# Hybrid decoder trunk, two layers on one core: four tiles for the samples' queries in place of two, and layer 0's compressed keys transposed later in the program

## The chip, the cores and the metric

The kernel runs as one program on one core of a Trainium2 chip. The metric is device time in microseconds (us), as the median of several executions. Durations and waits come from one profiled execution of the kernel before. Its engines: TensorE (PE, with its weight loads as PEld), VectorE (DVE), ScalarE (ACT), GpSimd (POOL) and SyncE (SP). SP issues the plain DMAs in program order, and a DMA that waits for its buffer holds back those behind it on SP; POOL issues the gathers in the same way.

## The reference, cut to what matters

One inference step through two layers, for one prompt of 512 rows and 8 samples of one row each, d_model 1024. In each layer:

- six modulation vectors per token group, `mod = silu(c) @ ada_w + ada_b` (the conditioning: shift1, scale1, gate1, shift2, scale2, gate2);
- `h = rms(x) * (1 + scale1) + shift1`, one projection `h @ w_in` into the columns of three groups of heads: forgetting attention (6 heads), sparse attention (6 heads, 2 key groups), pooling;
- the mixer, for the prompt over its own rows, for each sample over 2048 cached rows in pages;
- `o @ w_out`, a norm, a gate and the residual; then a squared-ReLU MLP of width 4096 in the same frame.

What the change touches is the samples' part of the mixer:

```python
# forgetting attention: s = q.k * SCALE + (cq - ck), softmax, p @ v over 2048 cached rows and the new one
# sparse attention, compressed branch:
kc, vc = blocks(kc_rows), blocks(vc_rows)      # mean of 64 cached rows each: 32 blocks per sample
s = einsum('btkgd,bnkd->btkgn', q5, kc) * SCALE
p = masked_softmax(s); o = p @ vc; imp = sum over the group's heads of p
idx = top 8 blocks by imp                      # these blocks are then attended to row by row
```

## The kernel before, in words

**Chains.** The program is written by generators that yield a cost after each step. `merge` (L118) keeps a virtual time per chain, the sum of its costs divided by its total (`Chain`, L97; the totals stand in L26), and always takes the next step from the chain furthest behind. A chain that yields `None` is blocked, and enters again at the others' virtual time. This sets the program order. A list scheduler with a modelled timeline then fixes the order on each engine: among what it takes to be ready, the earlier in the program goes first, and the `high_priority` blocks shift that (the conditioning's matmuls by 3000 places, the samples' chains by 300). On the chip each engine runs its list strictly in order. Tiles of one tag share a fixed number of buffers and get them in program order.

**Layer 0's chains that matter here.**
- `gemm_chain` (L826, total 506): 21 column tiles of the input projection, costs 5.3 and 0.45 each. `main` (L1548) then waits for the attention, does the second half of the output projection and the MLP in 8 chunks `c`.
- `fox_prompt` and `nsa_prompt`: the prompt's two attentions, on PE, DVE and ACT in alternation. `wout_first` (L1106) follows with the first half of the output projection.
- `ada0` (L1674, total 35): the conditioning parts 2 to 4, 48 weight loads of 256 KB (`wa`, two buffers, L292), each followed by a few matmuls `pada` (L268) and a cost of 0.25. Two loads share one accumulator in PSUM (L287).
- `cmp0` (L1681, total 70): `pre_cmp(0)` (L635) gathers 64 tiles of cached compressed keys and values (`cr`, POOL, L655), cost 0.2 each, and DVE sums them into two tiles `cg` (L645, L647; one tag, two buffers of 2 KB a partition). At its end it halves the sums, scales them to `kvc` (L666, L668), transposes the keys on PE into the PSUM tile `pkc` (L670, L672) and ACT copies them to `kct`.
- `sample` (total 120): `fox_sample` (L1209) takes 32 pairs of gathered tiles `fk` (POOL and DVE multiply with the query tile `qb`, L1230), four pairs to a sample, then `key_sample` (L1401), then the samples' output projection and MLP (`rows_of`).
- `nsa_sample` (L1320): starts, in the program, once `kct` is written; scores the compressed blocks (`psc`, L1331), ranks them and makes the gather indices `ixs` (`pix`, L1385), which `key_sample`'s gathers need.

**Shared buffers.** PSUM tag `n` is one bank. In layer 0 `ada0`'s `pada`, `pkc`, all of `nsa_sample`'s PSUM tiles, the samples' token-major copies and `wout_first`'s accumulators take it in turn, in program order:

```python
banks = dict(g=2, s=2, o=1, v=1, n=1, x=1)              # L172
acc = ps("pada", tag)                                   # L287, tag "n" from ada0
tag = "o" if l else "n"                                 # L639, in pre_cmp
p = ps("pkc", tag)                                      # L670
```

The SBUF tag `prod` (one buffer, so far 3 KB a partition) serves `lf` in `pre_lf` (L620), `scn` and `rr` in `nsa_sample`, the products in `key_sample` and a row copy in `rows_of`. The query tiles `qb` (L1205, 1.5 KB a partition) have two buffers; `load_q(b + 1)` (L1221) is issued on SP when sample b starts. `take` (L1187) lets the fox gathers run up to five tiles ahead (`RING`) once `kct` stands in the program, and three tiles before that, in layer 0. The gathered tiles `cr`, `fk`, `kt` and `st` share five buffers.

**Joining.** Chunks c = 0 to 3 of layer 0's MLP go without the samples' columns; from c = 4 on the samples are joined (L1576), and these chunks stand in the program behind the samples' own MLP rows. `fill` (L1666) then prepares layer 1: `pre_lf(1)`, `pre_cmp(1)`, where sums trail the gathers by three tiles.

Of the kernel before, what the change touches and what calls it, by code (L numbers as in the profile page):

```python
# [9 lines left out]
F32 = mybir.dt.float32  # L10
# [127 lines left out]
def trunk(ctx: ExitStack, tc: tile.TileContext, x_prompt, x_sample, cache_fox_kv, cache_fox_logf, cache_nsa_kv,  # L138
# [16 lines left out]
    wk = ctx.enter_context(tc.tile_pool(name="wk", bufs=2))  # L155
# [18 lines left out]
    def ps(name, tag="g"):  # L174
        return pp.tile([128, 512], F32, name=name, tag=tag, bufs=banks[tag])

    def acp(out, in_, scale=1.0):
        return S.activation(out, in_, AF.Copy, scale=scale)  # L178

    def ring(name, shape=(128, 1536), dt=F32):  # L180
        return big.tile(list(shape), dt, name=name, tag="ring", bufs=RING)
# [453 lines left out]
    def pre_cmp(l, room=lambda: True):  # L635

        tag = "o" if l else "n"  # L639
        trail = []  # L640

        def add(r, g, x):
            x = x.rearrange("p (r c) -> p r c", r=2)[:, :, 0:256]
            if r == 0:
                V.tensor_copy(ys[g], x)  # L645
            else:
                V.tensor_tensor(ys[g], ys[g], x, op=OP.add)  # L647

        ys = [wk.tile([128, 2, 256], F32, name="cg", bufs=2) for g in range(2)]
        for r in range(32):  # L650
            for g in range(2):
                while not room():
                    yield None
                x = ring("cr", (128, 1024))
                G.indirect_dma_start(out=x, out_offset=None, in_=nsa2,  # L655
                                     in_offset=bass.IndirectOffsetOnAxis(ap=idxc[:, l, g:g + 1], axis=0),
                                     element_offset=r * 1024)
                trail.append((r, g, x))
                if l == 0 or len(trail) > 3:
                    add(*trail.pop(0))  # L660
                yield
        for a in trail:
            add(*a)
        kvc = []
        for g in range(2):
            V.tensor_tensor(ys[g][:, 0], ys[g][:, 0], ys[g][:, 1], op=OP.add)  # L666
            y = wk.tile([128, 256], F32, name="kvc", bufs=2)
            V.tensor_scalar(y, ys[g][:, 0], 1.0 / 64, None, op0=OP.mult)  # L668
            kvc.append(y)
        p = ps("pkc", tag)  # L670
        for g in range(2):
            PE.transpose(p[:, g * 128:(g + 1) * 128], kvc[g][:, 0:128], ident)  # L672
        kct = wk.tile([128, 256], F32, name="kct", bufs=1)
        acp(kct, p[:, 0:256])
        pre[l]["kvc"], pre[l]["kct"] = kvc, kct
# [13 lines left out]
    def layer(l, X, hi, lo, rsw):  # L689
# [510 lines left out]
        qb = {}  # L1200

        def load_q(i):

            if i < 16:
                qb[i] = wk.tile([128, 384], F32, name="qb", bufs=2)  # L1205
                src = qscr[l][i % 8:i % 8 + 1, i // 8 * 384:i // 8 * 384 + 384]
                nc.sync.dma_start(qb[i], src.to_broadcast([128, 384]))

        def fox_sample():  # L1209
# [3 lines left out]
            to_tok([("fq", t) for t in range(3)], ztok[0:8, 0:384], "v")  # L1213
            nc.sync.dma_start(qscr[l][:, 0:384], ztok[0:8, 0:384])
            load_q(0)
            accm, todo = {}, []
            for n in range(32):
                b, j = divmod(n, 4)
                if j == 0:
                    if b < 7:  # L1220
                        load_q(b + 1)  # L1221
                    acc = ps("pvf", "v")
                    if b % 2 == 0:
                        nmS = wk.tile([66, 2, 4], F32, name="nmS", bufs=2)
                        lS = wk.tile([128, 2, 4, 6], F32, name="lS", bufs=2)
# [175 lines left out]
        def key_sample():  # L1401
# [7 lines left out]
            for b in range(8):  # L1409
                v = b % 4  # L1410
                if b == 0:
                    load_q(8)
# [253 lines left out]
        def fill():  # L1666
            while "joined" not in ready:
                yield None
            pre_lf(l + 1)
            yield 0.1  # L1670
            for _ in pre_cmp(l + 1):
                yield 0.3
# [6 lines left out]
            yield from ada(1, range(NB, 6), "n", hold=False)  # L1679

        def cmp0():  # L1681
            for _ in pre_cmp(0):
                yield 0.2

        ch_main = Chain(main(), W_G)
        chains = [ch_main, Chain(fox_prompt(), W_F), Chain(nsa_prompt(), W_N), Chain(pool_chain(), 12),
# [6 lines left out]
        if l == 0:  # L1693
            chains += [Chain(ada0(), W_A0), Chain(cmp0(), W_C0)]
# [17 lines left out]
    ys = ring("ys", (8, 1024))  # L1712
# [41 lines left out]
```

## Time and profile before

| | |
|---|---|
| Median of 3 runs | 1987.18 us (1971.4 to 1987.96) |
| Profiled execution: its time | 1987.2 us |
| Profiled execution: span from first to last instruction | 1985.4 us |
| PE busy in the span | 1823.3 us, 92% |
| Mean granted clock of PE | 0.933 |

A view by windows gives, for each stretch, the busy time of each engine with its number of instructions, the granted clock of PE as a share of 2.4 GHz (0.50 is the lower level, 1.2 GHz), and the busy share and rate of the DMA engines. A timeline row gives start, duration, engine, line, operation, output<-inputs, shapes and count, and in brackets the idle time of the engine ahead of it with what ended that. A view of waits gives who waited for whom: us in total, how often, the longest.

### The profile page before, as it was taken

The numbers are of one execution on the slowest core, as the hardware profiler recorded it, in microseconds if no ns is written. First come the engines' busy times: TensorE is split into PE (matmuls) and PEld (weight loads), VectorE is DVE, ScalarE is ACT, GpSimd is POOL, SyncE is SP. The second block draws the span as 40 slices with busy tenths as digits, with TensorE's granted clock in tenths as the row PEclk, the third lists the DMA queues.
The fourth block names the chain that finished last, engine by engine and source line by source line (L and its number), as shares of the span: only waits on it lengthen the run. The fifth ranks groups of instructions, "written<-read, shape, count | busy, mean of one in ns | idle before, by whom it ended". The sixth has DMA issues, their size and how long they took to land. (4 is left out here: it accounts for less than half of the span.)

```text
span 1985.4 us, 37190 instructions
## 1 busy us (share of the span) xinstructions
PE 1823.3 (92%) x13848; PEld 1434.9 (72%) x13848; DVE 1303.3 (66%) x3175; ACT 851.7 (43%) x1994; POOL 660.1 (33%) x542
## 2 busy tenths in 40 slices
PE   6999879897989899999998999979987999999998
PEld 3887745454648787679996787855665888878997
DVE  3678877666677684347667468896658778634555
ACT  3344535452334342233336344546655443423445
POOL 0535444224225550034340146355433655100000
PEclk9999957787989999999999999979998999999999
DMA  8979776457667667899996465545534776684332
GB/s 295 326 260 302 249 244 216 154 191 238 210 229 213 196 184 236 297 314 344 311 319 187 147 216 175 167 146 177 176 101 163 219 203 185 211 293 132 91 91 71
DMA packets 316024, 420.98 MB, mean 212 GB/s; under 512 B 28441, under 2 KB 233979, under 8 KB 315700
## 3 DMA queue, kind: packets, MB, share of 16 engines
q1 hardware_dynamic: 272324, 233.24, 38.0%
q0 software_dynamic: 43520, 185.36, 27.1%
q8 instruction: 110, 1.80, 0.4%
q14 instruction: 70, 0.57, 0.1%
HBM read 397.26 MB, written 21.44 MB: 211 GB/s over the span
## 5 line engine op out<-in xcount | busy, mean ns | idle before, releaser
L336 PE MATMUL pg<-ah,wh 128*128 128x262 f32 (+4 forms) x1792 | 542.9, 304 | 19.1 <-ACT wz L178 4.1
L336 PE MATMUL pg<-al,wh 128*128 128x262 f32 (+4 forms) x1792 | 536.9, 301 | 4.6 <-DVE al L526 2.9
L336 PE MATMUL pg<-ah,wl 128*128 128x260 f32 (+4 forms) x1792 | 535.1, 299 | 5.6 <-DVE wl L245 5.6
L178 ACT ACTIVATE wh<-wr 128x512 fp32r<-128x512 f32 x372 | 233.2, 629 | 437.1 <-PE pg L336 395.7
L336 PE MATMUL pg<-a,wh 128*128 128x262 f32 (+3 forms) x1664 | 379.1, 316 | 7.6 <-DVE a L1603 4.1
L336 PEld LDWEIGHTS pg<-ah,wh 128*128 128x128 f32 x1792 | 343.6, 192 | 49.8 <-issue 19.7
L336 PEld LDWEIGHTS pg<-al,wh 128*128 128x128 f32 x1792 | 343.0, 192 | 27.0 <-issue 9.5
L336 PEld LDWEIGHTS pg<-ah,wl 128*128 128x128 f32 x1792 | 344.2, 192 | 24.8 <-issue 9.9
L245 DVE TENSOR_TENSOR wl<-wr,wh 128x512 fp32r<-128x512 f32 x368 | 270.6, 737 | 110.0 <-ACT wh L178 107.7
L336 PEld LDWEIGHTS pg<-a,wh 128*128 128x128 f32 x1664 | 276.8, 191 | 40.8 <-issue 9.1
L336 PE MATMUL pg<-a,wl 128*128 128x258 f32 (+3 forms) x832 | 258.8, 312 | 0.9 <-DVE wl L245 0.9
L1230 POOL TENSOR_TENSOR fk<-fk,qb 128x768 f32<-128x768 f32 x96 | 182.9, 1909 | 229.6 <-DMA fk<-in_cache_fox_kv_dram,idxf 157.9
L655 POOL DMA_INDIRECT cr<-in_cache_nsa_kv_dram,idxc x128 | 130.1, 1017 | 308.4 <-PE prw L268 133.1
L485 POOL DMA_INDIRECT fk<-in_cache_fox_kv_dram,idxf x128 | 129.7, 1013 | 270.3 <-PE pvf L1238 97.9
L336 PEld LDWEIGHTS pg<-a,wl 128*128 128x128 f32 x832 | 158.5, 191 | 10.3 <-issue 2.5
L1615 DVE TENSOR_TENSOR F<-F,pg 128x258 f32<-128x258 f32 (+3 forms) x188 | 88.2, 473 | 116.6 <-PE pg L336 112.4
L1231 DVE TENSOR_REDUCE S<-fk 128x12 f32<-128x768 f32 x128 | 120.6, 943 | 24.9 <-POOL fk L1230 24.6
L485 POOL DMA_INDIRECT st<-in_cache_nsa_kv_dram,ixs x96 | 102.7, 1070 | 77.4 <-PE pvs L1444 45.3
L1597 ACT ACTIVATE rl<-rl,wb 128x256 f32<-128x256 f32 (+2 forms) x128 | 64.5, 506 | 134.5 <-DVE rl L1596 132.2
L268 PE MATMUL pada<-wa,cT 128*32 128x256 f32 x640 | 98.5, 426 | 21.2 <-DMA wa<-in_w_ada_dram 20.3
L178 ACT ACTIVATE P<-P,st 128x128 f32<-128x128 f32 (+3 forms) x144 | 78.3, 558 | 48.3 <-DVE st L889 23.7
L1652 POOL TENSOR_TENSOR xt<-xt,yt 128x512 f32<-128x512 f32 x2 | 2.5, 1270 | 281.2 <-DVE xt L1654 279.9
(438 smaller groups left out, 2851.9 us busy)
## 6 DMA issues: line engine op xcount, KB each, us to landing
wr<-in_w_ff_dram SPq DMA_DIRECT2D x256, 256.0 KB
wa<-in_w_ada_dram SPq DMA_DIRECT2D x160, 256.0 KB
wrow<-in_w_ff_dram SPq DMA_DIRECT2D x64, 512.0 KB
wr<-in_w_in_dram SPq DMA_DIRECT2D x80, 256.0 KB
out_dram<-kt SPq DMA_DIRECT2D x16, 512.0 KB
wrow<-in_w_out_dram SPq DMA_DIRECT2D x16, 512.0 KB
kt<-in_cache_nsa_win_dram SPq DMA_DIRECT2D x16, 448.0 KB
qb<-qscr SPq DMA_DIRECT2D x32, 192.0 KB
```

The lines of the kernel that those rows point to most:

```text
L178: return S.activation(out, in_, AF.Copy, scale=scale)
L245: V.tensor_tensor(lo, raw, hi.bitcast(F32), op=OP.subtract)
L268: PE.matmul(acc[c * 32:(c + 1) * 32, 0:256], rows[:, k, :], raw[:, (c % 2) * 256:(c % 2 + 1) * 256], start=first, stop=last)
L336: PE.matmul(acc[:, 0:b - a], wt, x(k)[:, a:b], start=n == 0, stop=n == 3 * nk - 1)
L485: G.indirect_dma_start(out=out, out_offset=None, in_=view, in_offset=bass.IndirectOffsetOnAxis(ap=idx, axis=0))
L655: G.indirect_dma_start(out=x, out_offset=None, in_=nsa2, in_offset=bass.IndirectOffsetOnAxis(ap=idxc[:, l, g:g + 1], axis=0), element_offs ...
L1230: (G if i == 0 or l else V).tensor_tensor(kk, kk, qb[b][:, None, :].to_broadcast([128, 2, 384]), op=OP.mult)
L1231: V.tensor_reduce(S4[:, 2 * i:2 * i + 2], kk.rearrange("p r (h d) -> p r h d", d=64), axis=AX, op=OP.add)
L1597: S.activation(r[:, a:e], r[:, a:e], AF.Relu, bias=st["wb"])
L1615: V.tensor_tensor(F[:, m, a:b], F[:, m, a:b], p[:, 0:b - a], op=OP.add)
L1652: G.tensor_tensor(xt[:, b, h], xt[:, b, h], t, op=OP.add)
```

## The change

The two tiles `cg` become the halves of one tile in the tag `prod`, whose buffer grows from 3 KB to 4 KB a partition. The query tiles get four buffers. `pre_cmp` yields once more, with a cost of 10, between the last sum and the halving; in layer 0 that cost counts (10/70 of virtual time), in layer 1 `fill` replaces it with its own 0.3.

```diff
-        ys = [wk.tile([128, 2, 256], F32, name="cg", bufs=2) for g in range(2)]
+        ys = wk.tile([128, 2, 2, 256], F32, name="cg", tag="prod", bufs=1)
+        ys = [ys[:, g] for g in range(2)]
         for r in range(32):
...
         for a in trail:
             add(*a)
+        yield 10
         kvc = []
         for g in range(2):
             V.tensor_tensor(ys[g][:, 0], ys[g][:, 0], ys[g][:, 1], op=OP.add)
...
-                qb[i] = wk.tile([128, 384], F32, name="qb", bufs=2)
+                qb[i] = wk.tile([128, 384], F32, name="qb", bufs=4)
...
         def cmp0():
-            for _ in pre_cmp(0):
-                yield 0.2
+            for c in pre_cmp(0):
+                yield c or 0.2
```

## Rows read from the trace of the kernel before

**Rows 1.** The page: busy time of PE, and the granted clock of PE in 40 slices of the span, in tenths.
```profile
PE 1823.3 (92%) x13848; PEld 1434.9 (72%) x13848; DVE 1303.3 (66%) x3175; ACT 851.7 (43%) x1994; POOL 660.1 (33%) x542
...
PEclk9999957787989999999999999979998999999999
```
**Rows 2.** Windows over four stretches of layer 0: length, then busy time and count of PE, PEld, DVE, ACT, POOL, then granted clock, DMA share and GB/s.
```profile
75.00:195.00 120.00, 119.95 (x943) 99.44 (x944) 95.97 (x257) 54.07 (x130) 50.31 (x44) 1.00 0.88 297
195.00:246.00 51.00, 45.62 (x372) 38.26 (x370) 40.91 (x107) 24.59 (x57) 24.06 (x20) 1.00 0.80 263
246.00:338.50 92.50, 74.40 (x395) 43.95 (x395) 70.87 (x191) 42.79 (x109) 40.63 (x37) 0.63 0.66 218
338.50:478.50 140.00, 121.61 (x771) 67.12 (x771) 86.48 (x229) 60.83 (x169) 46.12 (x36) 0.74 0.57 196
```
**Rows 3.** The same stretches for the instructions on the tile `pada` alone: busy time and count of PE, PEld, DVE, ACT, then clock, DMA share and GB/s of the whole core.
```profile
75.00:195.00 120.00, 11.29 (x80) 2.62 (x80) 4.13 (x10) 0.39 (x1) 1.00 0.88 297
195.00:246.00 51.00, 0.00 (x0) 0.00 (x0) 0.00 (x0) 0.00 (x0) 1.00 0.80 263
246.00:338.50 92.50, 0.00 (x0) 0.00 (x0) 0.00 (x0) 0.00 (x0) 0.63 0.66 218
338.50:478.50 140.00, 19.15 (x120) 4.08 (x120) 5.36 (x13) 0.77 (x2) 0.74 0.57 196
```
**Rows 4.** Timeline of PE, 335 to 348 us: the users of PSUM tag `n` in their order.
```profile
336.19 0.33 PE L672 MATMUL pkc<-cst,kvc 128*128 128x128 f32 x1
338.67 0.47 PE L672 MATMUL pkc<-cst,kvc 128*128 128x128 f32 x1 [2.15 <-DVE kvc L668]
...
341.07 0.84 PE L1126 MATMUL ptt<-cst,zs 128*8 128x128 f32 x3
...
344.49 1.11 PE L1331 MATMUL psc<-kct,qc 128*64 128x256 f32 x2
...
347.37 1.08 PE L268 MATMUL pada<-wa,cT 128*32 128x256 f32 x8
```
**Rows 5.** The matmuls of the conditioning that read `wa`, 0 to 195 us: count, minimum, median and longest in ns, first and last start in us.
```profile
L268 PE MATMUL pada<-wa,cT x104: 379/403/632, 51.0 to 191.5; 128*32 128x256 f32 x104
```
**Rows 6.** Timeline of DVE, 336 to 339 us: the end of the sums and what is made of them.
```profile
336.70 0.69 DVE L647 TENSOR_TENSOR cg<-cg,cr 128x512 f32<-128x512 f32 x1 [1.16 <-DMA cr<-in_cache_nsa_kv_dram,idxc]
...
338.33 0.28 DVE L668 TENSOR_SCALAR kvc<-cg 128x256 f32<-128x256 f32 x1
```
**Rows 7.** Waits of PE, 338.7 to 478.5 us: us in total, times, longest.
```profile
PE pada L268 <- DMA wa<-in_w_ada_dram: 10.0, 4, 4.9
PE psS L874 <- ACT P L888: 2.5, 3, 2.1
```
**Rows 8.** Timeline of PE: two of these waits.
```profile
395.79 0.63 PE L268 MATMUL pada<-wa,cT 128*32 128x256 f32 x4 [2.99 <-DMA wa<-in_w_ada_dram]
...
438.69 0.62 PE L268 MATMUL pada<-wa,cT 128*32 128x256 f32 x4 [1.81 <-DMA wa<-in_w_ada_dram]
```
**Rows 9.** Windows over three stretches at the lower clock: length, busy time and count of PE, PEld, DVE, ACT, POOL, then clock, DMA share, GB/s.
```profile
338.30:358.80 20.50, 19.82 (x76) 9.45 (x76) 11.94 (x34) 7.90 (x26) 6.51 (x5) 0.50 0.61 220
...
396.40:406.60 10.20, 10.20 (x56) 6.28 (x55) 2.57 (x10) 4.03 (x9) 2.87 (x3) 0.50 0.43 140
...
440.70:447.50 6.80, 6.80 (x41) 3.61 (x40) 3.61 (x8) 1.17 (x4) 0.45 (x1) 0.50 0.18 66
```
**Rows 10.** Waits of SP over the whole span for a buffer of `qb` (L1207): us in total, times, longest.
```profile
SPq L1207 <- DVE fk L1230: 66.5, 7, 47.5
...
SPq L1207 <- POOL fk L1230: 56.9, 5, 43.6
...
SPq L1207 <- DVE prod L1430: 18.0, 8, 3.2
```
**Rows 11.** Timeline of SP: the last load of `wa` ahead of the pause, the load of `qb` behind SP's longest wait for its buffer, and the next loads of `wa`.
```profile
192.95 1.53 SPq L293 DMA_DIRECT2D wa<-in_w_ada_dram  x1
...
342.44 0.36 SPq L1207 DMA_DIRECT2D qb<-qscr  x1
...
348.48 10.41 SPq L293 DMA_DIRECT2D wa<-in_w_ada_dram  x4
```
**Rows 12.** The fox multiplies of layer 0 on POOL, one to a pair, up to 340 us and from 340 to 600 us: count, ns, first and last start.
```profile
L1230 POOL TENSOR_TENSOR fk<-fk,qb x12: 1812/1824/2344, 109.1 to 328.7; 128x768 f32<-128x768 f32 x12
...
L1230 POOL TENSOR_TENSOR fk<-fk,qb x20: 1804/1818/2373, 343.4 to 573.6; 128x768 f32<-128x768 f32 x20
```
**Rows 13.** The indices for the samples' chosen blocks: made, and first used by a gather.
```profile
L485 POOL DMA_INDIRECT kt<-in_cache_nsa_kv_dram,ixs x16: 942/950/1427, 587.9 to 719.5; - x16
L1390 DVE TENSOR_SCALAR ixs<-pix,cst x1: 274/274/274, 416.5 to 416.5; 128x64 int32<-128x64 f32 x1
```
**Rows 14.** Layer 1's preparation: first sums of `cg`, the last reader of `lf`, and the first use of the transposed keys (last start of the row).
```profile
L645 DVE COPY cg<-cr x2: 419/420/421, 872.6 to 875.3; 128x512 f32<-128x512 f32 x2
...
L628 DVE TENSOR_TENSOR tt<-bi,lf x2: 202/206/209, 74.0 to 905.6; 128x48 f32<-128x48 f32 x2
...
L1331 PE MATMUL psc<-kct,qc x4: 379/530/686, 344.5 to 1238.8; 128*64 128x256 f32 x4
```
**Rows 15.** Where the samples' columns are put into the MLP's input (first of the two starts is layer 0), and the first evacuation with the samples joined.
```profile
L611 DVE TENSOR_TENSOR al<-catp,ah x2: 219/222/225, 800.2 to 1737.8; 128x64 fp32r<-128x64 f32 x2
...
L1599 ACT ACTIVATE rl<-pg x16: 155/158/160, 852.3 to 1041.1; 128x8 f32<-128x8 f32 x16
```

## The prediction

> **What bounds the kernel now.** I read the page first: PE is busy for 92% of the span, and its clock is full except in two places, of which layer 0's, around 250 to 480 us, is the larger [rows 1]. So time is won only where PE idles or runs at the lower clock. The windows show where: until 195 us PE is busy without a break at clock 1.00; from 246 to 338.5 us it idles for 92.5 - 74.4 = 18.1 us and has a mean clock of 0.63, from 338.5 to 478.5 us for 18.4 us at 0.74 [rows 2]. The reader is to see next what is missing there. The conditioning's matmuls on `pada`, which need nothing but their weights, run 20 loads in 75 to 195 us, none at all from 195 to 338.5 us, and 30 loads in the 140 us after that (4 matmuls a load) [rows 3]. The timeline says why: `pkc`, then the samples' query copy `ptt`, then `psc`, then `pada` again at 347.37 us, all on the one bank `n` and in program order [rows 4]. In the program `pkc` stands behind 64 gathers of 0.2 at a total of 70, at virtual time 0.183; `ada0` has then issued 0.183 x 35 / 0.25 = 25.6 loads, and the trace has 104 / 4 = 26 before the pause [rows 5]. On the chip the gathers end only at 336.7 us [rows 6]. So a transposition that nobody needs yet holds the bank for which PE's best filler waits, for 150 us.
>
> **The change part by part.** The profiled execution took 1987.2 us (span 1985.4 and 1.8 around it), the median is 1987.18, so sums stand against 1987.2 directly.
>
> *The later step.* A cost of 10 puts halving, scaling, transposition and all behind it at virtual time 0.183 + 10/70 = 0.326. `ada0` is then at 0.326 x 35 / 0.25 = 45.6 loads: 20 of its remaining 22 move ahead of `pkc`. What moves itself is small: four DVE instructions, two transposes, one ACT copy, and `nsa_sample` with its two stores on SP; no gather moves, since the cost comes after the last sum.
> 1. PE stands at `pkc` for 2.15 us because it reached it before the sums were done [rows 4, 6]. Later in the program it is taken when ready: -2.2 (ends: 0 and -2.2).
> 2. Twenty loads leave 338.5 to 478.5 us, where one costs 19.15 / 30 = 0.64 us: -12.8 (the two at 347.37 us took 1.08 us together, which would make 10.8). Ahead, at the pace of 75 to 195 us (one in 6 us, 11.29 / 20 = 0.56 us each), some 8 run in 195 to 246 us, where PE idles for 5.4 us, and 12 in 246 to 338.5 us, where it idles for 18.1 us. I charge 3 of the first 4.8 us and 2 of the other 6.5: +5.0 (ends: 0, all in gaps; +11.3, none).
> 3. With the burst gone its waits for weights go. Of the 10.0 us of such waits in the later stretch [rows 7], those at 395.8 and 438.7 us, 2.99 and 1.81 us, are `ada0`'s own [rows 8]: -4.8 (ends: 0, if they come back earlier; -10.0, if all four go).
> 4. Clock. Right behind these three waits of PE the lower level stands for 20.5, 10.2 and 6.8 us, in which PE is busy for 36.8 us [rows 9]; at 2.4 GHz that is 18.4 us less at most. Other waits, such as 2.5 us on `P`, remain there [rows 7], so I take half, 9.2. In 246 to 338.5 us the filler may lift the clock toward 0.74: 74.4 x (1 - 0.63 / 0.74) = 11 at most, of which I take 2. The later stretch loses filler and may fall toward 0.63: (121.6 - 12.8) x (0.74 / 0.63 - 1) = 19 at most, of which I take 3. Together -8 (ends: -29 and +19).
>
> The Trainium skill, "TensorE: Matmul & The Clock Gate", in Part 1 on the clock gate, says that the throttled state is the default and that activity releases it. The trace agrees: 1.00 in the stretch without gaps, 0.63 in the one with most. By that rule alone the clock term is a transfer of filler from one stretch to the other and its sum would be near 0, so 1974 in place of 1966.
>
> *Four query tiles.* With two, `load_q(b + 1)` waits on SP for the multiplies of sample b - 1: 141 us in all, the longest 47.5 us [rows 10]. That one stands from 295 to 342 us, with the next `wa` loads behind it [rows 11]. In the kernel before nobody misses them, because `pada` waits for bank `n` anyway: 0 by itself. In the changed kernel they are wanted just then, and two buffers would starve term 2 of some 8 loads (47 / 6). With four, a tile's last reader lies three samples back, so the wait is gone. Number and size of the loads stay the same.
>
> The Trainium skill, "DMA: Bandwidth & Descriptors", under "Issuing engines are not separate DMA queues", says that transfers issued by SP and by GpSimd share the same DMA engines and interleave. That speaks against the change: 12 loads of 256 KB are 3.1 MB more beside the gathers between 246 and 338.5 us, 14 us at the 218 GB/s measured there, while the DMA engines are 0.66 busy [rows 2]. By that rule the last sum comes some us later, which after the move holds up nothing on PE.
>
> *Three tiles ahead for longer.* `take` now runs three tiles ahead, not five, for (0.326 - 0.183) x 120 / 1.32 = 13 more pairs of `fox_sample`. Before 330 us, with three and with `cmp0`'s gathers between, a pair took (328.7 - 109.1) / 11 = 20.0 us; after 343 us, with five and alone, 230.2 / 19 = 12.1 us [rows 12]. No row separates the two causes: the ends are 0 and 13 x 7.9 = 103 us on the samples' chain. I expect near the lower end, since the five physical buffers stay and only the gathers' place in the program moves: +2 on PE.
>
> *The index chain.* `pix` now stands behind `wout_first`'s accumulators on bank `n` (its first step is at virtual time 0.389, `pix` at about 0.43). The indices are made at 416.5 us and first used at 587.9 us: 171 us of cover [rows 13]. `wout_first`'s work comes after 478.5 us and may push them past 540 us: 0, with some 40 us left.
>
> *The shared buffer.* In layer 1 the first sums, at 872.6 us, must now wait for the last reader of `lf` at 905.6 us, so the gathers stop after five: up to 33 us on them. The transposed keys made from them are first used at 1238.8 us [rows 14]: 0. In layer 0 the same order costs at most a few us at 60 us, before the pause: 0.
>
> Sum: -2.2 - 12.8 + 5.0 - 4.8 - 8 + 2 = -20.8, and 1987.2 - 20.8 = 1966.4. What is late next is the prompt's attention itself, through `P` and `psT`.
>
> **The rivals.**
> *A. The attention's own chain is the limit.* DVE and ACT alternate with PE in these stretches (DVE 0.77 and 0.62 busy [rows 2]). If PE's relief only widens its gaps, terms 2 to 4 come to 0 and 1985 remains. For it: PE waits on `P` in both. Against: PE is busy for 87% of the later stretch.
> *B. The samples come late (the slower side).* The samples' columns are ready at 800.2 us, and the first joined evacuation is at 852.3 us [rows 15]: 52 us of cover, 32 once the main path is 20 us earlier. Each us per pair on 13 pairs takes 13 us of it. Up to 2.5 us more a pair (14.6) nothing happens; at 4 (16.1) the gain is eaten; at 5.5 (17.6) the end is 20 us later than before, 2007. For it: 20.0 us in the stretch with three tiles. Against: half of the gathers on POOL there were `cmp0`'s.
> *C. The clock goes the other way.* By the rule on activity above, the later stretch, stripped of filler, falls to 0.63, and the earlier one gains nothing. From rows: -20.8 + 8 + 19 = +6, 1993. Against: two of the three stretches at the lower level begin where PE waited for weights of the filler itself.
> *D. It doesn't do what it says:* another user of bank `n` holds `pada` in place of `pkc`. Then terms 2 and 3 go, 1985 as in A; counted with it.
>
> **How the numbers follow.** Chances: forecast 0.53, A with D 0.27, B 0.12, C 0.08. The forecast's own range is 1945 to 1980, from halving and doubling its terms. What a measurement can tell from no change is about 1%, 20 us: below 1967.3 or above 2007.1. Of the forecast four fifths lie below: 0.42 faster. B lies above, beside the tails of A and C and an order of the whole program that the scheduler draws anew: 0.16 slower. The rest, 0.42, is within 1%. For the range, the good ends of all terms give -2.2 - 12.8 - 10 - 29 = -54, or 1933, which I don't expect together; I stop at 1939. Above it must hold A and C and reach into B: 2004.
>
> **What would show it.** Right: `pada` runs all through 195 to 338.5 us, and at most a few of `ada0`'s loads are left after `pkc`; no PE wait at `pkc`; the clock in 246 to 338.5 us is above 0.63; SP's waits for `qb` shrink to a few us; the output projection's first matmul (now 478.5 us) starts some 20 us earlier, and the first joined evacuation too. Wrong: `pada` still pauses (D); it doesn't, and 478.5 us stands all the same (A); the projection is early but the joined evacuation is not (B); the clock after 338.5 us is below 0.7 (C). What would refute the whole: a gain or loss that arises after 600 us, in stages that the change doesn't touch.

## The result: 1.2% slower, and the profile after

| | before | after |
|---|---|---|
| Median | 1987.57 us (4 runs, 1971.4 to 1997.07) | 2010.72 us (4 runs, 2005.39 to 2021.33) |
| Ratio, 95% interval | 1 | 1.0123 [1.0075, 1.0172] |
| Profiled execution, span | 1985.4 us | 2009.1 us |
| Mean granted clock | 0.933 | 0.926 |

The loss to the lower clock, span x (1 - mean clock), is 133 us before and 149 us after; what is left of the span is 1852 and 1860 us. This loss counts PE's idle time at the lower level too. Lines behind L665 lie two higher than before.

The page after, to [rows 1]: as many PE instructions; slices 6 to 12 (layer 0) are better, 16 and 18 (the join, as is seen below), 26 and 28 to 30 (layer 1) and the last worse.
```profile
PE 1841.2 (92%) x13848; PEld 1440.9 (72%) x13848; DVE 1291.6 (64%) x3175; ACT 856.3 (43%) x1994; POOL 666.4 (33%) x542
...
PEclk9999968899999996989999999877888999999998
```
Windows of layer 0 after, to [rows 2]:
```profile
195.00:246.00 51.00, 48.32 (x397) 39.30 (x395) 41.44 (x112) 24.47 (x59) 23.94 (x21) 1.00 0.91 306
246.00:338.50 92.50, 73.89 (x420) 41.25 (x421) 68.72 (x192) 41.75 (x108) 39.29 (x36) 0.70 0.74 249
338.50:478.50 140.00, 133.96 (x887) 84.42 (x886) 95.85 (x242) 76.11 (x195) 45.28 (x36) 0.92 0.59 198
```
The same for `pada` alone, to [rows 3]: 24 + 56 matmuls are 20 loads in what was the pause, and 19 are left in the last stretch.
```profile
195.00:246.00 51.00, 4.34 (x24) 1.08 (x24) 1.24 (x3) 0.00 (x0) 1.00 0.91 306
246.00:338.50 92.50, 10.63 (x56) 2.09 (x56) 2.48 (x6) 0.37 (x1) 0.70 0.74 249
338.50:478.50 140.00, 9.37 (x76) 2.34 (x76) 3.31 (x8) 0.38 (x1) 0.92 0.59 198
```
Timeline of PE after, to [rows 4]: `pkc` is taken without a wait, and the output projection's first matmul stands at 392.88 us, where it was 478.5.
```profile
344.17 0.69 PE L674 MATMUL pkc<-cst,kvc 128*128 128x128 f32 x2
...
349.89 0.42 PE L268 MATMUL pada<-wa,cT 128*32 128x256 f32 x4 [0.52 <-DVE scn L1336]
...
392.88 0.50 PE L336 MATMUL pg<-ah,wh 128*128 128x512 f32 x1
```
So the first part of the mechanism came, and larger than predicted: a lead of 85.6 us. From here on a tile is marked by the moment when ScalarE splits its weights for PE. The lead is 58 us at the MLP's first tile (544.1 to 486.0 us) and 81 us at the last tile of the first product in the MLP's chunk 3 (792.0 to 710.7 us). At the join, right behind that chunk, most of it is lost. First windows of before, then of after, around it:
```profile
700.00:750.00 50.00, 48.18 (x427) 43.28 (x425) 42.61 (x90) 20.62 (x46) 21.63 (x18) 1.00 0.68 193
750.00:800.00 50.00, 49.22 (x394) 38.02 (x395) 22.03 (x60) 13.97 (x33) 0.00 (x0) 1.00 0.71 229
800.00:850.00 50.00, 49.19 (x398) 33.03 (x397) 15.41 (x37) 10.99 (x22) 0.00 (x0) 1.00 0.90 304
850.00:900.00 50.00, 50.00 (x424) 40.41 (x423) 26.68 (x69) 19.87 (x44) 21.46 (x22) 1.00 0.95 321
```
```profile
700.00:750.00 50.00, 48.12 (x404) 42.58 (x404) 40.47 (x86) 20.02 (x47) 29.68 (x26) 1.00 0.68 201
750.00:800.00 50.00, 27.64 (x283) 16.47 (x281) 18.42 (x58) 3.19 (x12) 7.85 (x7) 0.69 0.67 228
800.00:850.00 50.00, 49.65 (x455) 35.69 (x451) 14.70 (x41) 17.44 (x41) 0.00 (x0) 1.00 0.95 332
850.00:900.00 50.00, 41.39 (x310) 31.63 (x306) 21.95 (x58) 7.68 (x15) 21.64 (x23) 0.86 0.78 269
```
After, PE idles 22.4 of the 50 us from 750 us on, at clock 0.69: the MLP has run up to the samples and has nothing to put between. Its last matmul ahead of the join starts at 752.00 us, the next, now with the samples, at 799.39. PE's timeline after shows what runs between, in brackets the idle time and what ended it: the samples' softmax and single loads of the conditioning.
```profile
763.58 0.42 PE L1142 MATMUL pmx<-cst,mx 128*66 128x128 f32 x1 [8.36 <-DVE mx L1137]
...
779.14 1.07 PE L268 MATMUL pada<-wa,cT 128*32 128x256 f32 x4 [3.19 <-DMA wa<-in_w_ada_dram]
...
794.62 0.64 PE L268 MATMUL pada<-wa,cT 128*32 128x256 f32 x2 [4.11 <-DMA wa<-in_w_ada_dram]
...
799.39 0.39 PE L336 MATMUL pg<-ah,wh 128*128 128x260 f32 x1
```
The samples' columns after, to [rows 15]: at 792.0 us, only 8 us sooner than before, and the first joined evacuation 15 us behind them, where it was 52.
```profile
L611 DVE TENSOR_TENSOR al<-catp,ah x2: 224/226/227, 792.0 to 1749.8; 128x64 fp32r<-128x64 f32 x2
...
L1601 ACT ACTIVATE rl<-pg x32: 154/156/158, 807.0 to 1964.1; 128x8 f32<-128x8 f32 x32
```
At layer 0's last tile 18.9 us of the lead are left (1058.95 to 1040.06). In layer 1 they turn into 21.0 us behind at the last tile of the output projection (1486.5 to 1507.5), and the end is 23.7 us late. Windows over layer 1's attention for the tile `pg` alone (input and output projection); the clock is that of the whole core. Before, then after:
```profile
1280.00:1340.00 60.00, 19.74 (x125) 16.87 (x124) 3.14 (x12) 0.32 (x2) 0.79 0.50 158
1340.00:1400.00 60.00, 6.55 (x21) 3.71 (x19) 0.00 (x0) 1.15 (x2) 0.96 0.55 188
1400.00:1460.00 60.00, 18.64 (x72) 12.97 (x72) 0.00 (x0) 2.94 (x5) 1.00 0.33 112
```
```profile
1280.00:1340.00 60.00, 12.26 (x57) 10.49 (x58) 1.60 (x6) 0.15 (x1) 0.67 0.44 141
1340.00:1400.00 60.00, 4.29 (x14) 2.45 (x13) 0.00 (x0) 0.58 (x1) 0.82 0.44 149
1400.00:1460.00 60.00, 13.68 (x53) 9.23 (x51) 0.00 (x0) 2.30 (x4) 0.81 0.29 97
```
Fewer projection matmuls stand beside the attention (124 in place of 218 over the three), and the clock is 0.67 to 0.82 in place of 0.79 to 1.00. A part of this is a shift: the input projection's last weights are split 20 us earlier than before (1299.6 to 1279.6 us), but the attention beside it came later. A matmul that stands in each of its score tiles shows this, before and after, in the first and last start:
```profile
L878 PE MATMUL psS<-cmb,identb x72: 216/229/289, 1159.8 to 1454.5; 128*128 128x128 bf16 x72
```
```profile
L880 PE MATMUL psS<-cmb,identb x72: 219/230/314, 1165.5 to 1474.1; 128*128 128x128 bf16 x72
```
So in layer 1 the lead is one of the projection and not of the attention, which ends 19.6 us later. Of the change only the query tiles are in use here: between 1100 and 1500 us SP waits 42.5 us for one on POOL's multiplies, before 55.6 us. The late step and the tile of the sums are done at 1044 us.

### The profile page after: what moved, and what is told of

Its sections match the earlier page's. It is cut to its first block, busy times and chain, and to the rows that moved or that the text cites. A ratio compares the mean times of both kernels' runs of the same rounds, so it can differ in the third digit from the quotient of the medians.

```text
span 2009.1 us, 37187 instructions
## 1 busy us (share of the span) xinstructions
PE 1841.2 (92%) x13848; PEld 1440.9 (72%) x13848; DVE 1291.6 (64%) x3175; ACT 856.3 (43%) x1994; POOL 666.4 (33%) x542
## 4 chain that ended last, share of the span: by engine, by line
PE 41%; DMA 7%; DVE 6%; issue 3%; POOL 3%; ACT 1%; SPq 0%; DVEq 0%; POOLq 0%; ACTq 0%
PE pg L336 28%; DMA fk<-in_cache_fox_kv_dram,idxf 2%; PE pada L268 2%; DMA wrow<-in_w_ff_dram 2%; PE prw L268 2%; PE ot L908 2%; DMA wa<-in_w_ada_dram 1%; POOL fk L1232 1%; PE psT L901 1%; PE psS L877 1%; DVE S L1233 1%; DVE wl L245 1%; DMA st<-in_cache_nsa_kv_dram,ixs 1%; PE psS L876 1%; PE pvf L1240 1%
## 5 line engine op out<-in xcount | busy, mean ns | idle before, releaser
L336 PE MATMUL pg<-ah,wl 128*128 128x262 f32 (+4 forms) x1792 | 535.0, 299 | 3.2 <-DVE wl L245 3.1
L245 DVE TENSOR_TENSOR wl<-wr,wh 128x512 fp32r<-128x512 f32 x368 | 275.4, 749 | 104.1 <-ACT wh L178 101.9
L1232 POOL TENSOR_TENSOR fk<-fk,qb 128x768 f32<-128x768 f32 x96 | 187.2, 1954 | 269.1 <-DMA fk<-in_cache_fox_kv_dram,idxf 197.8
L1617 DVE TENSOR_TENSOR F<-F,pg 128x262 f32<-128x262 f32 (+3 forms) x188 | 88.1, 473 | 82.7 <-PE pg L336 79.0
L908 PE MATMUL ot<-PT,wz 128*64 128x128 f32 x720 | 98.5, 322 | 2.4 <-ACT PT L178 2.3
```

What stands on the lines that cost most here:

```text
L245: V.tensor_tensor(lo, raw, hi.bitcast(F32), op=OP.subtract)
L336: PE.matmul(acc[:, 0:b - a], wt, x(k)[:, a:b], start=n == 0, stop=n == 3 * nk - 1)
L908: PE.matmul(ot[e * 64:(e + 1) * 64, i * 128:(i + 1) * 128], vs[e](j), PTs[e][:, j * 128:(j + 1) * 128], start=first and j == 0, stop=last ...
L1232: (G if i == 0 or l else V).tensor_tensor(kk, kk, qb[b][:, None, :].to_broadcast([128, 2, 384]), op=OP.mult)
L1617: V.tensor_tensor(F[:, m, a:b], F[:, m, a:b], p[:, 0:b - a], op=OP.add)
```

## The experiments

Theories: **M**, the mechanism just read (late step gives a lead, the join takes it, missing filler in layer 1); **Q**, the buffers cost the time; **S**, every edit makes the list scheduler draw another order, and what that order happens to do in the later stages outweighs the edit. The expectations are in us, with the kernel before at 1987. Runs 1 to 4, 5 to 8, 9 to 12, 13 to 16 and 17 to 18 are groups. In the first and the fourth every kernel, the one before too, took some 3% longer than in the others, so ratios are against the kernel before of the same group. "Loss" is the change of the lower clock's loss in us against it, "rest" that of the remaining span, both means.

| | ratio [95%] | loss | rest |
|---|---|---|---|
| 1 late step alone | 1.0012 [0.9977, 1.0047] | -2 | +5 |
| 2 both buffers alone | 1.0080 [1.0034, 1.0126] | +19 | -6 |
| 3 pause in layer 0 only | 1.0076 [1.0032, 1.0120] | +12 | 0 |
| 4 samples at 100 | 1.0049 [1.0008, 1.0090] | +15 | -4 |
| 6 the whole change | 1.0123 [1.0020, 1.0227] | +14 | +12 |
| 7 shared buffer alone | 1.0176 [1.0097, 1.0254] | +26 | +6 |
| 8 change, join at 7th block | 0.9965 [0.9924, 1.0005] | -6 | -1 |
| 9 shared buffer, `lf` apart | 1.0144 [1.0068, 1.0220] | +21 | +7 |
| 10 null: 505 for 506 | 1.0041 [0.9999, 1.0084] | +16 | -8 |
| 11 null: 121 for 120 | 0.9971 [0.9926, 1.0016] | +6 | -11 |
| 12 late step, join, 90 for 60 | 1.0022 [0.9990, 1.0054] | +2 | +5 |
| 13 shared buffer, first null | 1.0185 [1.0112, 1.0258] | +44 | 0 |
| 14 shared buffer, second null | 0.9975 [0.9931, 1.0019] | -1 | -2 |
| 15 change, first null | 1.0035 [0.9992, 1.0077] | +3 | +4 |
| 16 change, join, tag x | 0.9941 [0.9899, 0.9984] | -19 | +10 |
| 17 as 16 without the change | 1.0109 [1.0068, 1.0151] | +14 | +5 |
| 18 as 16, first null | 0.9995 [0.9951, 1.0039] | -10 | +6 |

**1. The late step alone** (kernel before, with)
```diff
+        yield 10
...
-            for _ in pre_cmp(0):
-                yield 0.2
+            for c in pre_cmp(0):
+                yield c or 0.2
```


> Only the late step: the pause of cost 10 ahead of the transposes in layer 0, two query tiles and two sum tiles as before. Theory M (the late transposes free the PSUM bank, the main path gets 60 to 90 us ahead, loses most of it where the samples join at c=4, and the early-spent products are missing beside layer 1's attention): 2000 to 2015 us, the output projection of layer 0 about 80 us earlier as in the changed kernel, PE idle in 750 to 800 us. Rival Q (four query tiles and the shared sum tile cost the time, in layer 1): 1955 to 1970 us. Rival S (each change of the order redraws the schedule, where it lands is no property of the edit): anywhere in 1970 to 2010 us.


The ratio is 1.0012, neither M's nor Q's. The lead is there (second half of the output projection's weights split at 447.9 us, 447.1 in run 3), with two query tiles; PE is busy for only 121.7 of the 150 us from 750 us on. So the lead is the step's, four tiles aren't needed for it, and in this order nothing of it is left at the end.

**2. The buffers alone**
```diff
-        ys = [wk.tile([128, 2, 256], F32, name="cg", bufs=2) for g in range(2)]
+        ys = wk.tile([128, 2, 2, 256], F32, name="cg", tag="prod", bufs=1)
...
-                qb[i] = wk.tile([128, 384], F32, name="qb", bufs=2)
+                qb[i] = wk.tile([128, 384], F32, name="qb", bufs=4)
```


> Only the four query tiles and the two sums in one tile of the shared buffer; the transposes where they were. M: 1980 to 1995 us, the conditioning pauses in 195 to 338 us as before and the output projection of layer 0 starts near 513 us. Q: 2005 to 2015 us, the loss arising in layer 1. S: 1970 to 2010 us with layer 0's markers as before.


The ratio is 1.0080, without a lead (the same marker stands at 510.6 us), and all of it is loss to the lower clock. That speaks for Q at this point; S allows it too.

**3. The pause in layer 0 alone** (changed kernel, with `if l == 0:` ahead of `yield 10`)


> The changed kernel with the pause of cost 10 in layer 0 alone; in layer 1 the compressed keys are made without it. M: layer 0 as in the changed kernel to within 5 us at every marker, layer 1's attention late again, 2000 to 2015 us. Q: the same, 2005 to 2015 us. S: layer 0 the same, but layer 1 differs by more than 10 us in either direction.


The ratio is 1.0076, within all theories. VectorE, ScalarE and GpSimd have the same instructions in the same order as in the changed kernel, so this is a repetition of it and tests nothing; against run 2 of the same group (1.0080) the late step again makes no difference.

**4. The samples' weight** (changed kernel, `W_S` 120 to 100)


> The changed kernel with the samples' chain given a weight of 100 in place of 120, so that its steps stand earlier in the program. M: the samples' columns of layer 0 (L613 to L616, ready at 792 us in the changed kernel) come before 770 us, PE is busy for more than 40 of the 50 us in 750 to 800 us (27.6 in the changed kernel), total 1985 to 2000 us. Q: no help in layer 1, 2005 to 2015 us. S: 1970 to 2010 us, not tied to the busy time in 750 to 800 us.


The ratio is 1.0049. The expectation has the sign wrong: a smaller total makes the chain's virtual time run faster, so its steps came later (samples' columns at 850.2 us, 823.3 in run 3). 27 us later and not slower: the samples' lateness at the join alone doesn't set the total.

**5, 6. The kernels before and after, once more**


> The kernel before, unchanged, for a profile on the chip of these runs. If the chip alone moved the first four (all 2050 to 2062 us with the kernel before at 2051), its markers lie as in the first profile, stretched by some 3%, with layer 0's output projection again some 60 us later than in the runs that have the late step, and the whole loss to the half clock near 160 us.

> The changed kernel on this chip. If the parts add (late step 1.0012, buffers 1.008 of the kernel before): ratio 1.005 to 1.013. Span less the loss to the half clock within 8 us of that of the kernel before, the loss 12 to 20 us larger, as the buffers alone showed. S (no property of the edit): a ratio anywhere in 0.99 to 1.015.


The kernel before took 1975.6 us in the one execution of run 5: the 3% were the group's, not the kernel's. The change is at 1.0123 again, with a loss 14 us larger, as expected, and a rest 12 us larger, where at most 8 was expected.

**7. The shared buffer alone** (kernel before, the first two lines of run 2's diff)


> Only the two sums in one tile of the shared buffer, two query tiles, no late step. If the shared buffer is what costs in the buffers' part (1.008): ratio 1.005 to 1.011, a mean granted clock below 0.917. If the four query tiles are it: ratio 0.997 to 1.003, clock 0.919 to 0.923.


The ratio is 1.0176, above both expectations and, within the intervals, at least as much as the whole change. **9.** takes `lf` out of the shared buffer:
```diff
-        lf = wk.tile([128, 8, 16, 6], F32, name="lf", tag="prod", bufs=1)
+        lf = wk.tile([128, 8, 16, 6], F32, name="lf", bufs=1)
```


> The sums in the shared buffer, but the gathered forget logs lf in a buffer of their own, so that layer 1's first sums need not wait for lf's last reader; otherwise as the run with the shared buffer alone (1.0176). If that wait is what costs: ratio 0.995 to 1.005, layer 1's sums begin near 872 us again. If the shared buffer costs elsewhere: 1.01 to 1.02. S (each new order lands somewhere): 0.995 to 1.02, with layer 1's sums early and no tie to the time.


Layer 1's first sums, in run 7 and then in run 9:
```profile
L645 DVE COPY cg<-cr x2: 419/419/419, 891.4 to 891.7; 128x512 f32<-128x512 f32 x2
```
```profile
L645 DVE COPY cg<-cr x2: 421/421/421, 857.3 to 857.6; 128x512 f32<-128x512 f32 x2
```
They come 34 us earlier, and the ratio is still 1.0144: the wait for `lf`, the one that the prediction names for this buffer, isn't needed for the loss.

**10, 11. Null changes** (`W_G` 506 to 505; `W_S` 120 to 121)


> A null change of the kernel before: the input projection's total cost 505 in place of 506 (0.2%), which gives each engine another order and nothing else. S: a ratio that differs from 1 by more than its interval, up to 1.015 above or below. M and Q, in which named resources cost the time: 0.997 to 1.003.

> A second null change of the kernel before: the samples' total cost 121 in place of 120 (0.8%). S: a ratio that differs from 1 by more than its interval, up to 1.015 either way, and not that of the first null. M and Q: 0.997 to 1.003.


The ratios are 1.0041 and 0.9971, neither apart from 1 by more than its interval, which S had expected; 1.0041 lies outside what M and Q allow, though its interval reaches into that. Yet both move loss and rest against each other, by +16 and -8, +6 and -11 us.

**13, 14. The shared buffer under the two nulls**


> The shared buffer alone (1.0176) with the first null change (input projection 505 in place of 506). If the shared buffer costs by itself, whatever the order: 1.012 to 1.022. S (the loss belongs to one drawn order): 0.995 to 1.012.

> The shared buffer alone with the second null change (samples 121 in place of 120). Shared buffer by itself: 1.012 to 1.022. S: 0.995 to 1.012, and another ratio than with the first null.


The ratios are 1.0185 and 0.9975. The buffers are the same, costs changed by 0.2% and 0.8%, and 2.1% lie between, with intervals far apart: sharing the buffer is not enough to cost anything, the order that comes with it decides (S). That sharing makes poor orders more likely (runs 7, 9 and 13 against 14) isn't excluded, and the four query tiles were never run alone. **15.** does it to the whole change:


> The whole change (1.0123) with the first null change (505 in place of 506). M, in which the stop at the join and the early-spent products cost the time: 1.008 to 1.017, with PE again idle for more than 15 of the 50 us at 750 to 800 us. S: 0.995 to 1.008.


The ratio is 1.0035, within S's range and not M's, but its interval overlaps that of run 3 (1.0032 to 1.0120), which has the order of the change; so this run leans to S and doesn't show it. The stop at the join is there still (PE busy for 128.9 of the 150 us from 750 us on), though not in the 50 us named.

**8. The join later** (changed kernel; the samples' rows of the MLP compute a third quarter by themselves)
```diff
-SQ = 2, 2
+SQ = 3, 2
```


> The changed kernel with layer 0's samples joined at the seventh and eighth column block in place of the fifth and later (a size: 3 and 2 rows of the schedule in place of 2 and 2), so that the main path meets the samples' chain later; it computes the samples' feed-forward for more blocks by themselves. M: PE no longer stops in 750 to 800 us (over 45 of the 50 us busy), the lead of layer 0's main path is kept to its end, total ratio 0.985 to 1.003. S: 0.995 to 1.015 and no relation to the stop.


The ratio is 0.9965. From 750 us PE no longer stops, and layer 1's first weights are split at 1001.5 us (1053.0 in run 6, 1060.2 in run 5, the kernel before); but there the conditioning isn't ready. First a window, then PE's wait for its loads between 1000 and 1200 us:
```profile
750.00:800.00 50.00, 49.35 (x480) 41.83 (x478) 29.56 (x76) 18.43 (x42) 4.62 (x4) 1.00 0.70 232
```
```profile
PE pada L268 <- DMA wa<-in_w_ada_dram: 18.9, 8, 6.0
```
**12.** tries to bring that forward by its total, on the late step alone (`SQ = 3, 2`, `W_A1` 60 to 90):


> A version: the late step alone (two query tiles, two sum tiles, ratio 1.0012), layer 0's samples joined at the seventh block (ratio 0.9965 with the whole change), and the total of layer 1's conditioning at 90 in place of 60, so that it stands earlier, since in the run with the later join PE waited for its weights at 1112 to 1150 us at half clock (47.8 us). M: 0.975 to 0.99, no stretch at half clock over 20 us in 1050 to 1200 us. S: 0.985 to 1.01.


The ratio is 1.0022, a miss: PE is at half clock for 44.4 us from 1133.6 us on. Behind its first 16 loads, done by 549 us, layer 1's conditioning went on no earlier than in run 8 (777.0 us; 770.7). **16.** takes away what holds it, the users of PSUM tag `s` that stand ahead of it in the program:
```diff
-            tag = "s" if "ff" in ready and feed["w"] % 2 else "x"
+            tag = "s" if l and "ff" in ready and feed["w"] % 2 else "x"
```


> A version: the whole change with the join at the seventh block (0.9965), and the samples' softmax steps of layer 0 on PSUM tag x alone in place of x and s in turn, so that layer 1's conditioning, on tag s, need not wait in program order for the end of the samples' keys (its first product came at 770 us, just as these end). M: the first product of layer 1's conditioning between 530 and 600 us, no half clock of 20 us and more in 1050 to 1200 us, ratio 0.975 to 0.99. S: 0.99 to 1.015.


Windows on `pada`, in run 8 and then in run 16:
```profile
525.00:750.00 225.00, 0.00 (x0) 0.00 (x0) 0.00 (x0) 0.00 (x0) 0.98 0.65 191
750.00:850.00 100.00, 7.78 (x72) 2.29 (x72) 0.00 (x0) 0.39 (x1) 1.00 0.79 266
850.00:1200.00 350.00, 41.67 (x248) 9.35 (x248) 0.00 (x0) 1.55 (x4) 0.90 0.86 293
```
```profile
525.00:750.00 225.00, 33.97 (x232) 7.85 (x232) 0.00 (x0) 1.54 (x4) 0.96 0.72 220
750.00:850.00 100.00, 15.93 (x104) 3.65 (x104) 0.00 (x0) 0.77 (x2) 0.95 0.64 201
850.00:1200.00 350.00, 0.00 (x0) 0.00 (x0) 0.00 (x0) 0.00 (x0) 0.98 0.83 275
```
It is done 300 us earlier, and no stretch at half clock beyond 10.2 us is left from 1050 to 1200 us. The ratio is 0.9941, its interval just below 1, and short of the 0.975 to 0.99 expected. **17, 18.** the same without the change, and under the first null:


> The version of the run before (0.9941) without the change: the join at the seventh block and the samples' softmax steps of layer 0 on tag x, on the kernel before (two query tiles, two sum tiles, no late step). If the late step's lead of 80 us is worth something once the join no longer eats it: 0.998 to 1.008 here, above 0.9941. If the lead is worth nothing: 0.988 to 0.997.

> The version (0.9941) with the first null change (505 in place of 506). If its gain comes from the two edits: 0.988 to 0.998. S, in which it is one more drawn order: 0.998 to 1.012.


Without the change the ratio is 1.0109, above even the 0.998 to 1.008 for a lead that is worth something. With the join out of the way the kernels with the late step and its buffers are thus 1.1 to 1.7% faster than the one without (0.9995 / 1.0109 and 0.9941 / 1.0109), and in the profiles of runs 17 and 18 the lead is there at layer 1's first weights (1081.2 to 1042.6 us). But that is one order against two, and between two orders 2.1% were seen: that the step is worth this is not shown. Under the null the ratio is 0.9995, as S expects: of the version's own gain over the kernel before, 0.6%, nothing is certain.

## Why the prediction was wrong

**Terms 1 to 4: right place, layer 0's gain sized too small.** The wait at `pkc` is gone. Ahead of it stand 46 of `ada0`'s loads (184 matmuls on `wa`), where 45.6 were forecast. Twenty loads ran in the pause, 6 + 14 where I had 8 + 12; the later stretch kept 19 of 30, so it lost 9.8 us of `pada`, not 12.8. That so many stayed has a plain reason: `ada0` takes parts 2 to 5 (`range(2, N5)` with `N5 = 6`), 64 loads and not 48, so 38 and not 22 remained behind the first 26, and 18 are still behind `pkc`. The stretch's waits for weights fell from 10.0 us [rows 7] by more than the forecast 4.8:
```profile
PE pada L268 <- DMA wa<-in_w_ada_dram: 2.6, 2, 2.2
```
The clock is the term that was mis-sized most: the loss is 92.5 x (0.70 - 0.63) = 6.5 us and 140 x (0.92 - 0.74) = 25.2 us less, 31.7 together, against -8 and a good end of -29. And the output projection came in beside the attention, which I had not seen: 85.6 us earlier, not 20.

The Trainium skill, "TensorE: Matmul & The Clock Gate", Part 1 on the clock gate, has activity release the throttled state. The trace agrees with it at both ends: 0.74 to 0.92 where the projection's matmuls came in, 0.79 to 0.67 in layer 1 where more than half of them are missing. The transfer between two stretches of layer 0 that I drew from it did not come: both rose (0.63 to 0.70, 0.74 to 0.92).

**Four query tiles: wrong, and not needed.** SP's waits for `qb` [rows 10] shrank from 141 to 95 us, not to a few (44.3 + 40.9 + 9.9, the last for `prod`):
```profile
SPq L1209 <- POOL fk L1232: 44.3, 6, 30.4
SPq L1209 <- DVE fk L1232: 40.9, 6, 25.5
```
Run 1 has two tiles, the same lead, and 23 loads in 195 to 338.5 us: term 2 was not starved of 8.

The Trainium skill, "DMA: Bandwidth & Descriptors", under "Issuing engines are not separate DMA queues", let me expect the last sum some us later. The trace agrees: it starts at 341.7 us, 336.7 before [rows 6], with DMA at 0.74 where it was 0.66. No run separates the shared engines from the new order here.

**Three tiles ahead: inside its ends.** The last fox multiply of layer 0 on POOL starts at 603.3 us, not 573.6 [rows 12], 30 us late. But the reason is another than the pace: in 480 to 620 us POOL waits 45.5 us with its gathers for the products `pvf`, which stand in PE's order behind the MLP's matmuls; before, it waited 20.1 us. First after, then before:
```profile
POOL fk L485 <- PE pvf L1240: 45.5, 4, 38.3
```
```profile
POOL fk L485 <- PE pvf L1238: 20.1, 3, 11.6
```
**Index chain and shared buffer: 0, as predicted,** in their waits. The indices come 40 us later (456.7 us) and are first used at 606.6. Layer 1's first sums wait for `lf` until 883.5 us [rows 14] and end at 1040.9 us, before at 1045.3.

**The rivals.** A was right on the attention (its last scores at 444.3 us, before 443.3) and wrong on what follows. B had the right place, the join, but not the price: the samples' columns weren't late (792.0 us, 800.2 before), the main path was early, and what the join takes is the lead, no more. C's clock fell, but in layer 1.

**What failed.** Two steps. The first: the sum carried what the middle of layer 0 wins straight to the end, with nothing charged at the join. It set the samples' 52 us of cover against a main path 20 us earlier. The main path was 81 us earlier, used up the cover, and PE stood at the join; 18.9 us of the lead were left at layer 0's end. Run 8 supports this: with the join one quarter of the MLP later PE no longer stops, and layer 1's first weights come 51 us sooner than in run 6.

The second is the sum's premise that the program keeps its order outside the edited steps, with "an order of the whole program that the scheduler draws anew" left unpriced in the 0.16. The sentence that was to refute the whole came true: from 18.9 us ahead at layer 0's end to 23.7 us behind, in stages of which the change touches only the query tiles. Runs 13 and 14 show how much an order can be worth: 2.1%, 42 us, twice the predicted gain; over all runs without the later join the ratio goes from 0.9971 to 1.0185. A range up to 2025 us would have followed from that.

For the orders that were drawn, the late step makes no difference at the end as the join stands (1.0012 alone, 1.0076 against 1.0080 with the buffers). What it is worth apart from the order is not shown. That the 1.2% belongs to the drawn order, and to no part of the change, is the likelier reading by runs 13 to 15; it stays open, since the shared buffer may favour poor orders, and no run shows which step of layer 1's order costs the time.

## What to carry to other kernels

Where a scheduler redraws the whole order at each edit, measure first what a null change of the order does, and give the range at least that width; an edit's own gain counts beyond it. Do it on the changed kernel too: the two nulls lie 0.7% apart on the kernel before and 2.1% on the one with the shared buffer. A lead is worth what the next meeting point lets through: ask where the faster chain has to wait for another, and move that point (here the join, and the PSUM tag that kept layer 1's conditioning behind the samples) together with the edit.

## What the hardware showed beyond that

- Between executions of one and the same kernel span and granted clock go together: in 24 runs of the kernel before (first group) the correlation is -0.82, and 0.01 of mean clock goes with 15 us.
- Between kernels too: over the 17 ratios of the table the correlation with the loss to the lower clock is 0.89, with the rest of the span 0.22. Most of what these edits win or lose stands in that loss; that the clock is its cause is not shown, since PE's idle time is in it.
- Whole groups of runs differed by 3% for all kernels, and the loss to the clock explains only a part: for the kernel before it was 160 us in the first group and 134 us in the second, the rest 1887 and 1850 us. No run shows what the rest of the 3% is.
